# Mask rows of a query tile on ScalarE, and three weight remainders on VectorE, both instead of GpSimd

## The chip, the core and the metric

One NeuronCore of a Trainium2 chip runs the whole kernel. The metric is the time of one execution on the device, in microseconds (us); lower is better. The engines are named as in the profile: PE is TensorE's matmul side and PEld its weight loads, DVE is VectorE, ACT is ScalarE, POOL is GpSimd and SP is SyncE, which issues most DMAs here. A q behind a name (SPq, POOLq) is that engine's instruction queue.

## What is computed

One layer of a decoder is applied to a prompt of 1024 tokens and, with the same weights, to 8 sample sequences of 4 new tokens each (32 rows). Cut to what matters here:

```python
h = rmsnorm(x, norm1_g)
q, kv, gn, u, mq, gb = in_proj(h, w_in)
# branch A: compressed blocks + selected blocks + sliding window, with ALiBi
s = einsum('bghtd,bgnd->bghtn', q, k) * dh ** -0.5 - slope * distance
o_a = gate0 * softmax(s_cmp) @ v_cmp + gate1 * softmax(s_sel) @ v_sel + gate2 * softmax(s_win) @ v_win
# branch B: state space scan; branch C: cross attention into 256 memory rows
x = x + (concat(o_a, o_b, o_c) * gb) @ w_o
def ffn(x, g, w1, w2):                 # w1: 1024 x 4096, w2: 4096 x 1024
    h = rmsnorm(x, g)
    return x + square(relu(h @ w1)) @ w2
```

The sample sequences read their selected rows out of a paged cache, through a page table. All arithmetic is fp32. A product is done as three matmuls on rounded parts: a value is split into a rounded "hi" and the remainder "lo = value - hi", and hi x hi, hi x lo and lo x hi are added up.

## The kernel before

The program is written stage by stage in Python and then put in order by a scheduler that simulates a timeline. It fixes one static order of instructions for each engine, and each engine works through its own list without overtaking, so an instruction that waits holds up all that stands behind it on the same engine.

The stages that the change touches are two.

**Attention, about 630 to 1060 us of the profile.** For each of 8 query tiles j of 128 tokens there is one unit of memory attention (`mem_unit`) and, for each of 2 key groups g, two units of prompt attention (`nsa_units`). The scores of a unit are S = QA·KA + mask + QB·KB, in the lines L839, L841 and L842. QA holds the rounded queries. QB has the remainders of the queries in its rows 0 to 63 (VectorE, L792), and in its rows 64 to 127 the mask rows that belong to the tile: constant rows `augq`, multiplied by a column of factors `augj` that selects the tile (L790). KB has the key positions in the same rows, so that the second matmul also adds the position bias. QA and QB have two buffers each, which the memory units share, so the next QB can be written only when PE has read the tile before the last one. DVE takes the row maximum (L847), ACT the exponential P (L848), DVE scales P (L880), PE transposes it (T, L893), ACT copies the transpose out (PT, L895), and PE multiplies with the values (O, L907).

Into the same stretch the scheduler weaves the attention of the sample sequences (`sample`). Its selected cache rows are gathered by indirect DMAs that POOL issues (L1338, tile `xs`, 512 KB each, 32 of them, 7 buffers), and PE transposes (L1497) and multiplies them (L1504, L1529).

**The start of the MLP, about 1220 to 1300 us.** After the output projection (L1668 adds its result into `acc`) the hidden input is split into h2hi (ACT, L1720) and h2lo (DVE, L1722), in 3 column chunks of 352 tokens by 8 slices. The MLP has 32 tiles m of 128 hidden units, 4 of them in the first group. For each m, `weights` loads one 128 x 1024 piece of w_ff1 (`raw`, 3 buffers, L1633), ACT rounds it to `hi` (L112) and L118 forms `lo`; PE computes 3 chunks of 24 matmuls each (`fps`, L122 to L124); ACT and DVE make the squared relu and split it (L1762 to L1765). A piece of w_ff2 is loaded into another `raw` buffer and split into f2hi (L112) and f2lo (L118). After m = 1, PE sums the squares of the norm (L1743), DVE rescales them (L1744), and PE transposes a part of them (L1779) before it goes on with m = 2.

The argument `e_lo` of `split` names the engine of the subtraction in L118: "pool" unless a caller says "dve". In the MLP only the w_ff1 piece of m = 0 goes to DVE; all other lo pieces of both matrices go to POOL.

Of the kernel before, what the change touches and what calls it, by code (L numbers as in the profile page):

```python
# [13 lines left out]
AF = mybir.ActivationFunctionType  # L14
ALU = mybir.AluOpType
# [8 lines left out]
KT = D // 128  # L24
# [77 lines left out]
class Build:  # L102
# [671 lines left out]
    def nsa_units(self, pool, psp, j, g):  # L774
        nc = self.nc
        ctx = {"n": 0, "total": (j + 1) + min(j + 1, 5) + 1}

        def prep():
            tk = slice(j * 128, j * 128 + 128)
            qd = pool.tile([128, 4, 128], F32, name="qd", tag="qd", bufs=3)  # L780
            for dd in range(2):
                nc.sync.dma_start(qd[dd * 64:(dd + 1) * 64], self.s_q[g * 256:(g + 1) * 256, tk].rearrange("(h d) t -> d h t", d=64))
            qd = qd.rearrange("p h t -> p (h t)")
            if g == 0:
                self._gn = pool.tile([128, 3, 8], F32, name="gn", tag="gn", bufs=2)
                nc.sync.dma_start(self._gn.rearrange("p b h -> p (b h)"), self.s_gn[tk])
            ctx["gn"] = self._gn
            QA = pool.tile([128, 512], R32, name="QA", tag="QA", bufs=2)
            QB = pool.tile([128, 512], R32, name="QB", tag="QB", bufs=2)
            nc.gpsimd.tensor_scalar(QB[64:128], self.augq[64:128, g * 512:(g + 1) * 512], self.augj[64:128, j:j + 1], None, op0=ALU.mult)  # L790
            nc.scalar.activation(QA, qd, AF.Copy, scale=0.125)
            nc.vector.scalar_tensor_tensor(QB[0:64], qd[0:64], 0.125, QA[0:64].bitcast(F32), op0=ALU.mult, op1=ALU.subtract)  # L792
            ctx["QA"], ctx["QB"] = QA, QB
            ctx["gb"] = pool.tile([128, 256], F32, name="ngb", tag="ngb", bufs=5)
            for a in range(2):
                nc.sync.dma_start(ctx["gb"][:, a * 128:(a + 1) * 128], self.s_gb[2 * g + a][:, j * 128:(j + 1) * 128])

        return [self.nsa_unit(pool, psp, j, g, b, ctx, prep if b == 0 else None, b == (0 if j < 7 else 1)) for b in range(2)]
# [925 lines left out]
    def ffn(self, rp, wp):  # L1724
        nc, A = self.nc, self.A
# [3 lines left out]
        with self.pool("ff") as pool, self.pool("ffp", PSUM) as psp:  # L1729
# [9 lines left out]
            def sum_ms():  # L1739
                for o, n in CHUNKS:  # L1740
                    cs = slice(o, o + n)
                    ps = psp.tile([128, 512], F32, name="fps", tag="fps", bufs=8)
                    nc.tensor.matmul(ps[:, :n], ones, ms[:, cs], start=True, stop=True)  # L1743
                    ts(ms[:, cs], ps[:, :n], 1.0 / D, EPS, op0=ALU.mult, op1=ALU.add)  # L1744
# [5 lines left out]
            for g0, NG in GROUPS:  # L1750
                hid = []
                for m in range(g0, g0 + NG):
                    mc = slice(m * 128, m * 128 + 128)
                    hi, lo = self.weights(wp, A["w_ff1"][0][:, mc], KT, "dve" if m == 0 else "pool")
                    yh = pool.tile([128, NT], R32, name="yh", tag="yh", bufs=4)
                    yl = pool.tile([128, NT], R32, name="yl", tag="yl", bufs=4)
                    for ci, (o, n) in enumerate(CHUNKS):
                        ps = psp.tile([128, 512], F32, name="fps", tag="fps", bufs=8)
                        for k in range(KT):
                            self.mm3(ps[:, :n], hi[:, k], lo[:, k], hhi[:, k, o:o + n], hlo[ci][:, k], k == 0, k == KT - 1)  # L1760
                        r = rp.tile([128, 512], F32, name="rl", tag="rl", bufs=2)[:, :n]
                        nc.scalar.activation(r, ps[:, :n], AF.Relu)  # L1762
                        tt(r, r, r, op=ALU.mult)  # L1763
                        nc.scalar.activation(yh[:, o:o + n], r, AF.Copy)
                        tt(yl[:, o:o + n], r, yh[:, o:o + n].bitcast(F32), op=ALU.subtract)  # L1765
                    raw2 = wp.tile([128, 8, 128], F32, name="raw", tag="raw", bufs=3)
                    hi2 = pool.tile([128, KT, 128], R32, name="f2hi", tag="f2hi", bufs=4)
                    lo2 = pool.tile([128, KT, 128], R32, name="f2lo", tag="f2lo", bufs=4)
                    nc.sync.dma_start(raw2.rearrange("p k c -> p (k c)"), A["w_ff2"][0][mc])
                    self.split(hi2, lo2, raw2)  # L1770
                    hid.append((yh, yl, hi2, lo2))
                    if m == 1:
                        sum_ms()
                        for i0 in (0, 8):
                            pm = psp.tile([128, 512], F32, name="fps", tag="fps", bufs=8)
                            r = rows(i0)
                            n = 8 if i0 == 0 else 1
                            for i in range(i0, i0 + n):
                                nc.tensor.transpose(pm[:r, (i - i0) * 32:(i - i0) * 32 + 32], ms[0:32, i * 128:i * 128 + r], ident[:32, :32])  # L1779
                            nc.vector.reciprocal(rm[:r, i0:i0 + n], pm[:r, 0:n * 32].rearrange("p (i c) -> p i c", c=32)[:, :, 0])  # L1780
                            stt(rm2[:r, i0:i0 + n], rm[:r, i0:i0 + n], 1.0 / D, rm[:r, i0:i0 + n], op0=ALU.mult, op1=ALU.mult)
                        for k in range(KT):
                            eng = nc.gpsimd if k >= 4 else nc.vector
                            eng.tensor_tensor(acc[:, k], acc[:, k], ms, op=ALU.mult)
                last = g0 + NG == 32
                steps = [(m, c) for c in LAST for m in range(KT)] if last else [(m, c) for m in range(KT) for c in CHUNKS]
                for si, (m, (o, n)) in enumerate(steps):
                    ps = psp.tile([128, 512], F32, name="fps", tag="fps", bufs=8)
                    for a, (yh, yl, h2, l2) in enumerate(hid):
                        self.mm3(ps[:, :n], h2[:, m], l2[:, m], yh[:, o:o + n], yl[:, o:o + n], a == 0, a == NG - 1)  # L1790
                    tt(acc[:, m, o:o + n], ps[:, :n], acc[:, m, o:o + n], op=ALU.add)  # L1791
                    if last and si in NORMS:
                        self.final_norm(pool, wp, psp, NORMS.index(si), rm, rm2, gf)
# [70 lines left out]
```

## Time and profile before

| | |
|---|---|
| median of 3 runs | 1992.77 us (1992.62 to 1998.18) |
| profiled execution | 1998.81 us, of which the span of the profile is 1997.0 us |
| PE busy | 1898.1 us (95%) |
| DVE busy | 1145.0 us (57%) |
| ACT busy | 754.5 us (38%) |
| POOL busy | 433.7 us (22%) |
| granted TensorE clock, mean | 0.976 of full speed |

The time of a profiled execution is its span plus about 1.8 us around it. An engine's share of the span is a mean over stages with different limits; whether its work counts is read from the stretch where it lies. "[6.66 <-DMA xs]" in a row means that the engine was idle for 6.66 us before this instruction and that a DMA into xs ended that. The granted clock has two levels that matter here, 1.2 and 2.4 GHz; in a stretch of time the profile gives the mean as a share of the higher.

### The profile page before, as it was taken

To read this page: it belongs to the slowest core of one execution; us is meant where nothing else is said; L and a number is where in the kernel's file an instruction comes from. 1 tells how busy PE (TensorE), PEld (TensorE's weight loads), DVE (VectorE), ACT (ScalarE), POOL (GpSimd) and SP (SyncE) were. 2 spreads that over 40 slices of the span, in tenths; PEclk is the share of its full clock that TensorE was granted. 3 is DMA by queue.
4 is the path that set the end of the run, shared out by engine and by line. 5 is a ranking of instruction groups with operands and counts; after the bars stand their busy time and mean duration, and the time that the engine had idled before them with its cause. 6 is when DMAs were issued, how large, how long until landed. Compare 5 with 4: busy or idle time off the path is not lost.

```text
span 1997.0 us, 33847 instructions
## 1 busy us (share of the span) xinstructions
PE 1898.1 (95%) x13280; PEld 1727.4 (86%) x13280; DVE 1145.0 (57%) x2735; ACT 754.5 (38%) x1696; POOL 433.7 (22%) x282
## 2 busy tenths in 40 slices
PE   8988999999997898989998999999999999999997
PEld 8987889999996665666657899999999999999997
DVE  6378897425535776786774226725455555544536
ACT  6301224226655666766774224212222111222222
POOL 2044431441102320022000122512121111122200
PEclk9988999999998799999999999999999999999999
DMA  7443323655336643433323223112111111111102
GB/s 267 150 132 91 102 79 102 180 178 181 117 114 136 182 143 95 144 95 108 107 75 121 70 80 96 53 32 64 43 43 53 43 43 43 43 44 52 43 1 87
DMA packets 197689, 191.31 MB, mean 96 GB/s; under 512 B 32925, under 2 KB 177046, under 8 KB 196314
## 3 DMA queue, kind: packets, MB, share of 16 engines
q1 hardware_dynamic: 190730, 153.86, 25.9%
q0 software_dynamic: 6800, 35.30, 5.3%
q8 instruction: 104, 1.70, 0.4%
q14 instruction: 55, 0.45, 0.1%
HBM read 155.34 MB, written 38.55 MB: 97 GB/s over the span
## 4 chain that ended last, share of the span: by engine, by line
PE 79%; DVE 9%; DMA 5%; issue 3%; ACT 2%; SPq 1%; POOL 1%; DVEq 0%; ACTq 0%; POOLq 0%
PE fps L122 12%; PE fps L124 12%; PE fps L123 12%; PE pso L122 4%; PE pso L124 4%; PE pso L123 4%; PE O L907 4%; PE T L893 3%; PE ops L124 2%; PE ops L122 2%; PE ops L123 2%; PE S L842 2%; PE S L839 2%; DMA xs<-cache_slc_kv,idx 1%; PE cps L632 1%
## 5 line engine op out<-in xcount | busy, mean ns | idle before, releaser
L1791 DVE TENSOR_TENSOR acc<-fps,acc 128x352 f32<-128x352 f32 (+3 forms) x336 | 173.4, 523 | 166.4 <-PE fps L124 166.3
L123 PE MATMUL fps<-h2lo,hi 128*128 128x352 f32 x768 | 249.0, 324 | 3.3 <-DVE h2lo L1722 3.3
L124 PE MATMUL fps<-h2hi,lo 128*128 128x352 f32 x768 | 249.5, 325 | 0.0
L122 PE MATMUL fps<-h2hi,hi 128*128 128x352 f32 x768 | 249.0, 325 | 0.0
L123 PE MATMUL fps<-yl,f2hi 128*128 128x352 f32 (+3 forms) x768 | 245.2, 322 | 0.0
L124 PE MATMUL fps<-yh,f2lo 128*128 128x352 f32 (+3 forms) x768 | 245.1, 322 | 0.0
L122 PE MATMUL fps<-yh,f2hi 128*128 128x352 f32 (+3 forms) x768 | 241.8, 323 | 0.0
L1763 DVE TENSOR_TENSOR rl<-rl 128x352 f32<-128x352 f32 x96 | 127.0, 1323 | 136.9 <-ACT rl L1762 136.9
L118 POOL TENSOR_TENSOR lo<-raw,hi 128x1024 fp32r<-128x1024 f32 (+1 forms) x43 | 96.8, 2252 | 378.0 <-ACT hi L112 378.0
L124 PE MATMUL pso<-hhi,wlo 128*128 128x352 f32 x480 | 157.8, 329 | 0.0
L123 PE MATMUL pso<-hlo,whi 128*128 128x352 f32 x480 | 157.6, 328 | 0.0
L122 PE MATMUL pso<-hhi,whi 128*128 128x352 f32 x480 | 157.5, 328 | 0.0
L118 POOL TENSOR_TENSOR f2lo<-raw,f2hi 128x1024 fp32r<-128x1024 f32 x32 | 77.6, 2429 | 349.9 <-ACT f2hi L112 294.4
L123 PEld LDWEIGHTS fps<-h2lo,hi 128*128 128x128 f32 x768 | 145.8, 190 | 4.1 <-DVE h2lo L1722 4.1
L848 ACT ACTIVATE P<-S,nst 128x384 f32<-128x384 f32 (+4 forms) x264 | 127.1, 488 | 57.9 <-DVE nst L847 46.8
L124 PEld LDWEIGHTS fps<-h2hi,lo 128*128 128x128 f32 x768 | 146.3, 190 | 0.0
L122 PEld LDWEIGHTS fps<-h2hi,hi 128*128 128x128 f32 x768 | 145.8, 190 | 0.1
L847 DVE TENSOR_REDUCE nst<-S 128x1 f32<-128x384 f32 (+4 forms) x264 | 109.5, 433 | 62.5 <-PE S L842 47.5
L123 PEld LDWEIGHTS fps<-yl,f2hi 128*128 128x128 f32 x768 | 144.0, 188 | 1.4
L124 PEld LDWEIGHTS fps<-yh,f2lo 128*128 128x128 f32 x768 | 143.9, 188 | 1.4
L122 PEld LDWEIGHTS fps<-yh,f2hi 128*128 128x128 f32 x768 | 143.2, 188 | 1.5
L112 ACT ACTIVATE f2hi<-raw 128x1024 fp32r<-128x1024 f32 x32 | 33.7, 1058 | 271.9 <-PE fps L123 255.6
(596 smaller groups left out, 4529.5 us busy)
## 6 DMA issues: line engine op xcount, KB each, us to landing
raw<-w_ff SPq DMA_DIRECT2D x64, 512.0 KB
wraw<-w_in SPq DMA_DIRECT2D x28, 512.0 KB
xs<-cache_mem_kv SPq DMA_DIRECT2D x16, 512.0 KB
s_gb<-st SPq DMA_DIRECT2D x36, 176.0 KB
x<-x_prompt SPq DMA_DIRECT2D x8, 512.0 KB
wraw<-w_mem_kv SPq DMA_DIRECT2D x8, 512.0 KB
qd<-s_q SPq DMA_DIRECT2D x32, 128.0 KB
ngb<-s_gb SPq DMA_DIRECT2D x64, 64.0 KB
```

The costliest lines, as they stand in the source:

```text
L118: eng.tensor_tensor(lo, src, hi.bitcast(F32), op=ALU.subtract)
L122: mm(ps, ahi, bhi, start=start, stop=False)
L123: mm(ps, ahi, blo, start=False, stop=False)
L124: mm(ps, alo, bhi, start=False, stop=stop)
L839: nc.tensor.matmul(S[:, :w], ctx["QA"][:, qs], KA[:, k0:k0 + w], start=True, stop=False)
L842: nc.tensor.matmul(S[:, :w], ctx["QB"][:, qs], KB[:, k0:k0 + w], start=False, stop=True)
L847: nc.vector.tensor_reduce(t[:, 0, pi, i:i + 1], S[:, o:o + pw], axis=AX.X, op=ALU.max, negate=True)
L848: nc.scalar.activation(P[:, o:o + pw], S[:, o:o + pw], AF.Exp, bias=t[:, 0, pi, i:i + 1], accum_out=t[:, 1, pi, i:i + 1])
L893: nc.tensor.transpose(T[:w, i * 128:(i + 1) * 128], Ps[i, si][:, o:o + w], self.ident)
L907: nc.tensor.matmul(O[c * 64:(c + 1) * 64, :256], v, pv[:w, c], start=n == 0, stop=n == total - 1)
L1763: tt(r, r, r, op=ALU.mult)
L1791: tt(acc[:, m, o:o + n], ps[:, :n], acc[:, m, o:o + n], op=ALU.add)
```

## The change

Two things move off POOL. The 16 multiplications of L790 become ACT instructions (a copy with a scale per partition). And three subtractions of L118 become DVE instructions: lo of the w_ff1 piece m = 1, and f2lo of the w_ff2 pieces m = 0 and m = 1.

```diff
@@ nsa_units, prep
-            nc.gpsimd.tensor_scalar(QB[64:128], self.augq[64:128, g * 512:(g + 1) * 512], self.augj[64:128, j:j + 1], None, op0=ALU.mult)
+            nc.scalar.activation(QB[64:128], self.augq[64:128, g * 512:(g + 1) * 512], AF.Copy, scale=self.augj[64:128, j:j + 1])
             nc.scalar.activation(QA, qd, AF.Copy, scale=0.125)
@@ ffn
-                    hi, lo = self.weights(wp, A["w_ff1"][0][:, mc], KT, "dve" if m == 0 else "pool")
+                    hi, lo = self.weights(wp, A["w_ff1"][0][:, mc], KT, "dve" if m < 2 else "pool")
@@ ffn
-                    self.split(hi2, lo2, raw2)
+                    self.split(hi2, lo2, raw2, e_lo="dve" if m < 2 else "pool")
```

The scheduler makes a new order from this for all engines in the attention stretch and at the start of the MLP; before the attention the order is the same. On POOL, in the attention stretch, with the gathers written as `DMA xs`:

```order
-L790 TENSOR_SCALAR QB<-augq,augj 64x512
-L1451 TENSOR_TENSOR xs<-xs,tri 128x900
-L1338 DMA xs<-cache_slc_kv,idx_7260 128x1024 x3
-L790 TENSOR_SCALAR QB<-augq,augj 64x512 x2
-L118 TENSOR_TENSOR w0lo<-mxr,w0hi 128x1024
-L1338 DMA xs<-cache_slc_kv,idx_7260 128x1024 x4
-L790 TENSOR_SCALAR QB<-augq,augj 64x512 x2
-L1338 DMA xs<-cache_slc_kv,idx_7260 128x1024 x8
-L790 TENSOR_SCALAR QB<-augq,augj 64x512 x2
-L1338 DMA xs<-cache_slc_kv,idx_7260 128x1024
-L790 TENSOR_SCALAR QB<-augq,augj 64x512 x2
```

These eleven rows are gone; in their place the gathers stand one behind another (13 in a row, and 16 later), with only L1451 and one w0lo between them.

On ACT, around one of the query tiles, the order before is

```order
L848 ACTIVATE P,nst<-S,nst 128x128
L791 ACTIVATE QA<-qd 128x512
L1347 ACTIVATE KTs<-sS 128x512
L895 ACTIVATE PT<-T 128x512
L895 ACTIVATE PT<-T 63x512
L791 ACTIVATE QA<-qd 128x512
L508 ACTIVATE P,nst<-S,nst 128x256 x4
```

and of the changed kernel, at the same tiles,

```order
L791 ACTIVATE QA<-qd 128x512
L790 ACTIVATE QB<-augq,augj 64x512
L848 ACTIVATE P,nst<-S,nst 128x128
L1347 ACTIVATE KTs<-sS 128x512
L895 ACTIVATE PT<-T 128x512
L895 ACTIVATE PT<-T 63x512
L791 ACTIVATE QA<-qd 128x512
L790 ACTIVATE QB<-augq,augj 64x512
```

Each L790 stands right behind the L791 of its tile (only the first tile has it ahead), and exponentials and copies out of PSUM stand behind it.

On DVE, at the start of the MLP (h2lo_14251 is the third column chunk), as a difference from before to after:

```order
 L1722 SCALAR_TENSOR_TENSOR h2lo_14251<-acc,g2c,h2hi 128x352
 L1737 MEMSET ones 128x128
+L118 TENSOR_TENSOR f2lo<-raw,f2hi 128x1024
+L118 TENSOR_TENSOR lo<-raw,hi 128x1024
+L118 TENSOR_TENSOR f2lo<-raw,f2hi 128x1024
 L1722 SCALAR_TENSOR_TENSOR h2lo_14251<-acc,g2c,h2hi 128x352
 L1674 TENSOR_TENSOR msb<-msb,rl 128x352
-L1763 TENSOR_TENSOR rl<-rl 128x352 x2
+L1763 TENSOR_TENSOR rl<-rl 128x352
+L1744 TENSOR_SCALAR msb<-fps 128x352 x2
```

The three subtractions stand behind 16 of the 17 h2lo instructions that are left after the output projection's last sums, ahead of the last one, and two of the three rescalings L1744 have moved ahead. On PE, two of the three sums L1743 now stand among the matmuls of m = 1 instead of behind them; the third, and the transposes L1779, stay behind.

## Rows read from the trace of the kernel before

**Rows 1.** Stretches 620 to 960 (sum) and 1350:1900: us, busy per engine, clock, DMA

```profile
sum 340.00, PE 308.15 PEld 218.06 DVE 248.82 ACT 223.84 POOL 68.65; mean PE 9.06 PEld 6.41 DVE 7.32 ACT 6.58 POOL 2.02
...
1350.00:1900.00 550.00, 550.00 (x3443) 550.00 (x3442) 285.33 (x433) 115.79 (x192) 115.21 (x49) 1.00 0.16 47
```

**Rows 2.** Waits of PE, 620 to 1070: us in total, times, longest

```profile
PE S L842 <- POOL QB L790: 9.5, 2, 7.2
PE S L839 <- ACT P L848: 7.4, 6, 3.4
PE O L907 <- ACT PT L895: 6.3, 10, 1.5
...
PE sS L1497 <- DMA xs<-cache_slc_kv,idx: 2.5, 3, 1.5
```

**Rows 3.** Timeline, 742 to 762: start, us, engine, line [idle before <- what ended it]

```profile
746.69 0.94 POOL L1338 DMA_INDIRECT xs<-cache_slc_kv,idx  x1 [0.30 <-PE S L842]
...
755.87 3.22 POOL L790 TENSOR_SCALAR QB<-augq,augj 64x512 fp32r<-64x512 bf16 x2 [8.24 <-issue]
...
757.49 0.63 PE L842 MATMUL S<-KB,QB 128*128 128x320 f32 x1 [7.24 <-POOL QB L790]
```

**Rows 4.** Gathers into xs, and the timeline 660 to 690

```profile
DMA to landing us min/median/max: 5.6/6.8/8.8
...
678.62 3.22 POOL L790 TENSOR_SCALAR QB<-augq,augj 64x512 fp32r<-64x512 bf16 x2 [6.66 <-DMA xs<-cache_slc_kv,idx]
```

**Rows 5.** Stretches of 10 us, columns as in the second of Rows 1

```profile
650.00:660.00 10.00, 9.11 (x55) 8.28 (x56) 7.76 (x42) 5.14 (x27) 0.00 (x0) 0.50 0.23 51
...
750.00:760.00 10.00, 2.76 (x14) 2.46 (x13) 4.00 (x13) 2.80 (x9) 3.13 (x2) 0.73 0.49 123
760.00:770.00 10.00, 10.00 (x91) 6.26 (x89) 4.83 (x14) 7.00 (x23) 0.00 (x0) 0.92 0.00 0
```

**Rows 6.** L790 (ns min/median/max), its wait for PE; ACT's L791 and its wait

```profile
L790 POOL TENSOR_SCALAR QB<-augq,augj x16: 1563/1566/1959, 629.5 to 994.0; 64x512 fp32r<-64x512 bf16 x16
...
  PE S L842: 69.0, 3
...
L791 ACT ACTIVATE QA<-qd 128x512 fp32r<-128x512 f32 x16 | 10.1, 632 | 8.1 <-PE S L839 3.6 <-DMA qd<-s_q 2.0 <-PE S L124 1.0
...
ACT QA L791 <- PE S L839: 3.6, 5, 1.5
```

**Rows 7.** Timeline of DVE and POOL, 1195 to 1300

```profile
1217.27 1.23 DVE L118 TENSOR_TENSOR lo<-raw,hi 128x1024 fp32r<-128x1024 f32 x1 [4.16 <-ACT hi L112]
...
1228.25 11.42 DVE L1722 SCALAR_TENSOR_TENSOR h2lo<-acc,g2c,h2hi 128x352 fp32r<-128x352 f32 x10
...
1240.03 2.06 DVE L1722 SCALAR_TENSOR_TENSOR h2lo<-acc,g2c,h2hi 128x352 fp32r<-128x352 f32 x4
...
1232.55 5.26 POOL L118 TENSOR_TENSOR f2lo<-raw,f2hi 128x1024 fp32r<-128x1024 f32 x2
```

**Rows 8.** Timeline of PE: first matmul of m = 0 to the first of m = 2

```profile
1227.61 0.32 PE L122 MATMUL fps<-h2hi,hi 128*128 128x352 f32 x1
...
1256.92 1.94 PE L1743 MATMUL fps<-msb,ones 128*128 128x352 f32 x6
...
1261.63 0.40 PE L1779 MATMUL fps<-ident,msb 32*128 32x32 f32 x4 [2.35 <-DVE msb L1744]
1261.96 0.43 PE L122 MATMUL fps<-h2hi,hi 128*128 128x352 f32 x1
...
1264.27 0.49 PE L124 MATMUL fps<-h2hi,lo 128*128 128x352 f32 x1
```

**Rows 9.** Stretch 1235:1240, columns as in the second of Rows 1

```profile
1235.00:1240.00 5.00, 2.77 (x9) 2.33 (x10) 5.00 (x6) 0.00 (x0) 2.80 (x2) 0.60 0.65 193
```

**Rows 10.** Load of the w_ff1 piece m = 2 issued, and its rounding on ACT

```profile
1232.62 0.38 SPq L1633 DMA_DIRECT2D raw<-w_ff  x1
...
1247.50 1.05 ACT L112 ACTIVATE hi<-raw 128x1024 fp32r<-128x1024 f32 x1
```

## The prediction

> **What bounds the kernel now.** The views are read from the coarse to the fine: the windows first, to see where PE is full and where it is not, then the waits of PE in the places where it is not, then the timeline at those waits. In the bulk of the MLP PE is busy for 550.00 of 550 us [rows 1], at about 0.160 us a matmul (550 / 3443); nothing that POOL, ACT or DVE do there can move the time. Between 620 and 960 us PE is busy for 308.15 of 340 us [rows 1], so 32 us are open, and at the start of the MLP PE waits again. The change touches just these two places. The reader should see that POOL is far from full in both (68.65 of 340 us) and still matters: not for its busy time, but because another engine stands behind it.
>
> In the attention stretch the longest single reason for PE to wait is POOL's L790: 9.5 us in two waits, of 7.2 us and 2.3 us [rows 2]. The timeline shows how the long one comes about. POOL has issued four gathers, the last at 746.69, and its next instruction is L790, which starts only at 755.87; PE stands for 7.24 us until the QB is there [rows 3]. A gather takes 5.6 to 8.8 us from issue to landing [rows 4], and 746.69 + 8.8 = 755.5: L790 starts just as the last gather is in. At 678.62 the same is said outright, L790 is released by the landing of a gather [rows 4]; this is the place of PE's other wait, the 9.5 - 7.2 = 2.3 us of [rows 2]. So L790 waits for gathers whose data it does not read, because it stands behind them on POOL.
>
> At the start of the MLP the bound is DVE, and behind it POOL. From 1228.25 ten h2lo instructions take 11.42 us, 1.14 each, where four of the same shape take 2.06, 0.51 each, a little later [rows 7]. The slow ones lie under POOL's subtractions: two f2lo run from 1232.55 for 5.26 us [rows 7]. PE waits for h2lo in that time; in 1235 to 1240 it is busy for 2.77 of 5 us, at a granted clock of 0.60, while DVE shows 5.00 of 5 [rows 9].
>
> **Part 1: L790 from POOL to ACT.** Removed are 16 instructions of 1.57 us on POOL [rows 6], 25 us that lie beside other work, and with them the two waits of PE, 2.3 + 7.2 = 9.5 us. On ACT the multiplication has no gather ahead of it. Behind the long wait PE also runs slower: the granted clock is 0.73 over 2.76 busy us and 0.92 over 10 [rows 5], which costs 0.27 x 2.76 + 0.08 x 10 = 1.5 us that goes with the wait. What is late next at these places? Behind the L842 at 757.49 PE has transposes of cache rows whose gathers are older than the four that L790 waited for, so I expect no wait of like size there. Gain: **11.0 us**, bounds 0 (another wait takes its place) and 11.0.
>
> Added are 16 instructions on ACT. The trace has none of this form there; the nearest row is L791, 632 ns for 512 columns [rows 6]. That is 16 x 0.63 = 10 us of busy time on an engine that is busy for 223.84 of 340 us [rows 1]. The Trainium skill, "ScalarE: Activation LUTs", section What ACT_TABLE_LOAD costs, gives 186 ns + 0.833 ns a column and 93 ns more for an operand of one value per partition, 0.71 us here; by it the busy time would be 11 us and the sum 0.1 to 1.4 us worse, and no row of L790 on ACT is there to check it.
>
> Each L790 also waits for PE to have read the old QB, and exponentials and copies stand behind it on ACT. On POOL that wait was 69.0 us in 3 cases and hurt nobody [rows 6]. L791 on ACT waits for the same tile's other buffer, 3.6 us in 5 cases, 1.5 at most [rows 6], and L790 stands right behind it, so most of its wait has passed by then. PE's own waits for ACT's two outputs are 7.4 + 6.3 = 13.7 us [rows 2], 6% of ACT's 223.84 busy us, so of 10 us more on ACT some 0.6 us would come through; to that I add as much again as L791 waits now, at most 3.6 us, and take 60% of it. Cost: **3 us**, bounds 0 and 10 + 3.6 = 14.
>
> POOL's queue is shorter for the gathers. That is worth little: a gather waits mostly for PE to free one of the 7 buffers. I take 0. The new order of the whole stretch is a term of its own, since the scheduler shuffles exponentials, transposes and gathers. I take 0 for it and 6 us either way, about as much as the other waits of rows 2 without ACT's larger one (6.3 + 2.5 = 8.8) could shrink or grow by two thirds.
>
> Attention: -11 + 3 = **-8 us**, from -17 to +9.
>
> **Part 2: three subtractions from POOL to DVE.** From its first matmul of m = 0 at 1227.61 to the first of m = 2 at 1261.96 PE takes 34.35 us [rows 8]. Its work there is 144 matmuls x 0.160 = 23.0 us, and 1.94 us of sums and about 0.9 us of transposes [rows 8], 25.9 in all. So 8.4 us are lost; and after the last wait, 2.35 us, matmuls of m = 2 start 0.29 us apart for about 12 instances (0.49 us each in [rows 8]) instead of 0.16, another 1.5 us. The pot is 9.9 us.
>
> With the change POOL has nothing to do there until pieces of m = 2 are split. DVE then needs 16 h2lo and 2 sums of 0.51 us, 9.2 us from 1228.25, to 1237.5. The three subtractions follow, 1.23 us each by the one that DVE did at 1217.27 [rows 7], 3.7 us, to 1241.2, and the last h2lo to 1241.7, where before it ended at 1246. PE, if it never waits, reaches the first matmul with lo of m = 1 after 76 matmuls and two sums, at 1227.6 + 12.2 + 1.3 = 1241.1, and lo is there at 1240.0; it reaches the last h2lo's matmul at about 1244, and that is there at 1241.7. So the chain just keeps up, and the third sum, its rescaling and the transposes end near 1254 instead of 1262. Cover: the raw buffers are freed later, near 1239 instead of 1232.6, so the next w_ff1 piece is loaded about 6 us later; before, it lay from 1232.62 to 1247.50 before ACT rounded it [rows 10], 15 us, so there is room. If that cover is gone, PE waits for lo of m = 2, by my count 2 us away. Gain: **8 us**, bounds 9.9 and a loss of 3.7 (see the third rival).
>
> **Sum.** -8 - 8 = -16 us against the profiled execution's own 1998.8 us: 1982.8. The median of the runs is 6.0 us under that execution. If these 6 us lie elsewhere, the median becomes 1976.8; if the quicker runs are those in which gathers land sooner and PE waits less for L790, they are part of the gain and it stays at 1982.8. I take the middle, **1980 us**.
>
> **Rivals.** First, a gather takes the place of L790. PE waits for gathers already, 2.5 us in 3 waits [rows 2], and if the prompt's tiles come sooner the transposes of cache rows do too, against an unchanged 6.8 us. Then part 1 nets about zero and part 2 remains: 1993 - 8 + 3 = 1988. For it speaks that all three waits follow the same pattern; against it, that the rows behind the long wait read older gathers.
>
> Second, slower: ACT's queue. If the wait of L790 for the old QB falls on ACT while exponentials stand behind it, PE loses it 16 times. At L791's worst wait of 1.5 us [rows 6] the price is 16 x (0.63 + 1.5) = 34 us, against a gain of 11 + 8 = 19: 2008. It decides from 19 / 16 = 1.2 us per multiplication, its own time included. For it speaks the 69.0 us of waiting on POOL; against it, that in the new order L790 stands behind L791, whose mean wait is 0.7 us in 5 of 16 cases.
>
> Third, DVE is simply full. It shows 5.00 of 5 us [rows 9]. If POOL is not what stretches h2lo, three more subtractions make the chain 3.7 us longer: -8 + 3.7, or 1989. Against it stands that h2lo takes 0.51 us wherever POOL rests and 1.14 beside it [rows 7]. The Trainium skill, "Perfetto Trace Analysis", section Optimizing Scalar/DVE Operations, advises to move work to GpSimd where DVE is saturated, and adds that the two share a port, so that moving between them might not help; by the first half this part loses 3.7 us, and these rows speak for the second half, with DVE's time stretched, not filled.
>
> Fourth, the clock gains more. The early attention runs partly at the lower level: from 650 to 660 PE is busy for 9.11 us at 0.50 of the full clock [rows 5], 4.6 us lost. If the new order leaves fewer gaps ahead of two such stretches, 9 us more are saved: 1971.
>
> That the change would not do what it says is excluded by the order: the multiplications are on ACT and the subtractions on DVE.
>
> **Chances.** Forecast 0.60; gather 0.15; ACT's queue 0.10; full DVE 0.08; clock 0.07. A measurement of this kernel can tell 0.3%, 6 us, from no change. Faster by more, under 1986.8: 0.60 + 0.07 + a fifth of the gather's case, 0.70. Slower by more, over 1998.8: 0.10. Between: 0.20. The range for 8 in 10: its lower end is the forecast less 6 us for the order and 9 us for the clock, 1965; its upper end takes in the gather's case and that of the full DVE with 3 us more of the order's term, 1992. Left out are ACT's queue and the tails.
>
> **What would show it.** Right, for part 1: no row in which PE waits for QB at more than 1 us, and gathers on POOL that follow one another; the wait of ACT's L790 for PE under 5 us in total. Right, for part 2: the ten h2lo at about 5.2 us instead of 11.4, and under 28 us between the first matmul of m = 0 and the first of m = 2. Wrong: PE's waits for P or PT from ACT grow by more than 5 us, PE waits for xs in place of QB, or POOL's pieces of m = 2 come after PE needs them.

## The result, and the profile after

The changed kernel takes 1978.49 us (median of 5 runs, 1975.86 to 1982.21) against 1992.77 us before (1991.86 to 1998.18). The medians are 14.3 us apart, a ratio of 0.9928; the ratio estimated from all runs is 0.9918, with a 95% interval of 0.9896 to 0.9939, which is 16.3 us. Ratios below are of this second kind. The forecast was 1980, from 1965 to 1992. The profiled execution took 1978.21 us, its span is 1976.4; before, span 1997.0. The two profiles differ by 20.6 us, more than the medians, because the profiled execution of before is slower than its median.

The program falls into four stretches with the same work in each kernel: the attention, from the first score matmul that reads a QB to the first matmul of the output projection; the projection; the MLP's start, from the first fps matmul of m = 0 to the first of m = 2; the rest. Here are the first and third in the windows view, of before and then of after (start:end, length, busy time and instructions of PE, PEld, DVE, ACT, POOL, granted clock, share and GB/s of DMA).

```profile
646.60:1070.00 423.40, 391.47 (x3266) 261.39 (x3263) 311.18 (x1018) 288.57 (x883) 64.10 (x50) 0.95 0.38 115
1227.61:1261.96 34.35, 28.68 (x161) 26.86 (x160) 31.56 (x37) 14.20 (x25) 18.29 (x8) 0.90 0.32 96
```

```profile
645.50:1054.10 408.60, 386.79 (x3266) 256.43 (x3265) 307.44 (x1018) 298.27 (x898) 38.06 (x34) 0.97 0.38 118
1212.18:1241.36 29.18, 25.83 (x162) 24.75 (x160) 26.11 (x39) 13.85 (x24) 8.60 (x4) 1.00 0.33 99
```

PE has the same 3266 matmuls in the attention and is done 14.8 us sooner: 10.1 us less idle (31.9 to 21.8) and 4.7 us less busy time at a higher granted clock. The MLP's start is 5.2 us shorter. The projection takes 157.6 and 158.1 us, the rest 735.04 us in both, so nothing is given back later; the last 1.1 us lie ahead of the attention.

The waits of PE in the attention of after (engine, line, waited for: us in total, times, longest), to be held against [rows 2]:

```profile
PE O L907 <- ACT PT L895: 6.1, 11, 1.2
PE T L893 <- DVE P L880: 4.6, 3, 3.2
PE S L839 <- ACT P L508: 3.2, 4, 1.3
PE S L839 <- ACT P L848: 3.0, 5, 0.8
PE sS L1497 <- DMA xs<-cache_slc_kv,idx: 2.0, 2, 1.0
```

No wait for QB is left, and the wait for P from L848 has fallen from 7.4 to 3.0 us, its longest from 3.4 to 0.8. New are 2.8 us for P from DVE's L880 (1.8 before) and 1.9 for P from L508 (1.3 before). L790 itself, in the view of one line of after (ns min/median/max, first and last start), answers [rows 6]:

```profile
L790 ACT ACTIVATE QB<-augq,augj x16: 716/717/720, 638.0 to 981.5; 64x512 fp32r<-64x512 bf16 x16
```

ACT stood idle ahead of none of the 16, and nobody waited more than 0.2 us for one.

At the MLP's start, the timeline of after (start, us, engine, line [idle before <- what ended it]) answers [rows 7 and 8]:

```profile
1212.82 5.04 DVE L1722 SCALAR_TENSOR_TENSOR h2lo<-acc,g2c,h2hi 128x352 fp32r<-128x352 f32 x10
...
1221.76 1.17 DVE L118 TENSOR_TENSOR f2lo<-raw,f2hi 128x1024 fp32r<-128x1024 f32 x1
1222.83 1.22 DVE L118 TENSOR_TENSOR lo<-raw,hi 128x1024 fp32r<-128x1024 f32 x1
1223.96 1.23 DVE L118 TENSOR_TENSOR f2lo<-raw,f2hi 128x1024 fp32r<-128x1024 f32 x1
...
1238.15 2.39 DVE L1765 TENSOR_TENSOR yl<-rl,yh 128x352 fp32r<-128x352 f32 x1 [0.80 <-ACT yh L1764]
1240.46 0.51 DVE L1744 TENSOR_SCALAR msb<-fps 128x352 f32<-128x352 f32 x1
```

```profile
1237.81 2.35 POOL L118 TENSOR_TENSOR f2lo<-raw,f2hi 128x1024 fp32r<-128x1024 f32 x1 [3.05 <-ACT f2hi L112]
```

```profile
1236.50 0.75 PE L1743 MATMUL fps<-msb,ones 128*128 128x352 f32 x2
1237.19 0.49 PE L1779 MATMUL fps<-ident,msb 32*128 32x32 f32 x5
1241.03 0.40 PE L1779 MATMUL fps<-ident,msb 32*128 32x32 f32 x4 [3.35 <-DVE msb L1744]
1241.36 0.54 PE L122 MATMUL fps<-h2hi,hi 128*128 128x352 f32 x1
```

The ten h2lo take 5.04 us instead of 11.42, the three subtractions 1.2 us each, and PE goes from m = 0 to the sums without a wait. One wait remains, and it has grown from 2.35 us [rows 8] to 3.35: the third sum's rescaling (L1744) stands on DVE behind an L1765 of 2.39 us, which lies under POOL's f2lo of m = 3 (1237.81 to 1240.16). Behind it the clock is low again, as before:

```profile
1241.36:1246.00 4.64, 4.64 (x21) 4.64 (x20) 4.64 (x2) 0.00 (x0) 4.64 (x2) 0.63 0.66 206
```

### The profile page after: what moved, and what is told of

The parts are those of the page before. It is cut to its first block, busy times and chain, and to the rows that moved or that the text cites. A ratio compares the mean times of both kernels' runs of the same rounds, so it can differ in the third digit from the quotient of the medians.

```text
span 1976.4 us, 33827 instructions
## 1 busy us (share of the span) xinstructions
PE 1889.7 (96%) x13280; PEld 1719.3 (87%) x13280; DVE 1139.4 (58%) x2738; ACT 764.8 (39%) x1712; POOL 399.1 (20%) x263
## 4 chain that ended last, share of the span: by engine, by line
PE 78%; DVE 9%; DMA 5%; ACT 3%; issue 2%; SPq 1%; POOL 1%; DVEq 0%; ACTq 0%; POOLq 0%
PE fps L122 12%; PE fps L124 12%; PE fps L123 12%; PE pso L122 4%; PE pso L124 4%; PE pso L123 4%; PE O L907 4%; PE T L893 4%; PE ops L124 2%; PE ops L122 2%; PE ops L123 2%; PE S L842 2%; PE S L839 2%; PE cps L632 1%; PE cps L122 1%
## 5 line engine op out<-in xcount | busy, mean ns | idle before, releaser
L1763 DVE TENSOR_TENSOR rl<-rl 128x352 f32<-128x352 f32 x96 | 127.0, 1324 | 134.4 <-ACT rl L1762 134.3
L118 POOL TENSOR_TENSOR lo<-raw,hi 128x1024 fp32r<-128x1024 f32 (+1 forms) x42 | 94.9, 2261 | 399.5 <-ACT hi L112 399.5
L118 POOL TENSOR_TENSOR f2lo<-raw,f2hi 128x1024 fp32r<-128x1024 f32 x30 | 71.9, 2399 | 377.0 <-ACT f2hi L112 331.3
L848 ACT ACTIVATE P<-S,nst 128x384 f32<-128x384 f32 (+4 forms) x264 | 127.9, 490 | 44.0 <-DVE nst L847 34.4
```

Source lines behind the costliest of these rows:

```text
L118: eng.tensor_tensor(lo, src, hi.bitcast(F32), op=ALU.subtract)
L848: nc.scalar.activation(P[:, o:o + pw], S[:, o:o + pw], AF.Exp, bias=t[:, 0, pi, i:i + 1], accum_out=t[:, 1, pi, i:i + 1])
```

## The experiments

Medians, ratios to the kernel before on the same chip, and the two stretches of the profiled execution:

| kernel | us (runs) | ratio, 95% | attention | m = 0 to 2 |
|---|---|---|---|---|
| before | 1991.5 to 1994.0 in four comparisons | | 423.4 | 34.3 |
| the change | 1978.5 (5) | 0.9918, 0.9896 to 0.9939 | 408.6 | 29.2 |
| part 1 alone | 1980.8 (6) | 0.9942, 0.9928 to 0.9956 | 406.1 | 34.3 |
| part 2 alone | 1988.8 (12) | 0.9977, 0.9962 to 0.9991 | 418.3 | 29.2 |
| L790 on DVE | 1991.2 (12) | 0.9985, 0.9970 to 1.0000 | 419.1 | 29.8 |
| L790 twice on ACT | 1981.8 (6) | 0.9948, 0.9928 to 0.9968 | 410.8 | 29.9 |
| POOL multiplies too | 1982.8 (6) | 0.9956, 0.9939 to 0.9973 | 411.7 | 29.5 |
| DVE multiplies too | 1975.5 (6) | 0.9919, 0.9901 to 0.9937 | 405.1 | 29.3 |
| POOL subtracts too | 1981.8 (6) | 0.9944, 0.9927 to 0.9962 | 405.8 | 34.7 |
| transposes later | 1976.2 (6) | 0.9921, 0.9904 to 0.9938 | 404.6 | 24.7 |
| backlog 12, POOL | 1989.1 (12) | 0.9979, 0.9966 to 0.9993 | 416.8 | 29.4 |
| backlog 12, ACT | 1980.5 (6) | 0.9929, 0.9915 to 0.9943 | 406.9 | 29.7 |
| backlog 16, POOL | 1990.5 (12) | 0.9985, 0.9972 to 0.9997 | 419.7 | 29.6 |
| backlog 16, ACT | 1975.7 (5) | 0.9907, 0.9891 to 0.9923 | 404.9 | 29.8 |

### Each part alone

Part 1 alone:

```diff
-                    hi, lo = self.weights(wp, A["w_ff1"][0][:, mc], KT, "dve" if m < 2 else "pool")
+                    hi, lo = self.weights(wp, A["w_ff1"][0][:, mc], KT, "dve" if m == 0 else "pool")
...
-                    self.split(hi2, lo2, raw2, e_lo="dve" if m < 2 else "pool")
+                    self.split(hi2, lo2, raw2)
```

> Part 1 alone (L790 on ACT; the three subtractions of the MLP's start back on POOL). Theory A, that the two parts do not touch each other: the stretch from the first score matmul with QB to the first matmul of the output projection takes 408.6 us as in the changed kernel (423.4 before), and from the first fps matmul of m = 0 to the first of m = 2 it takes 34.3 us as before, so about 1978.5 + 5.2 = 1983.7 us, 9 us faster than before. Rival B, that part 1 is worth only what PE lost by its two waits for QB less my price for ACT, 8 us, and part 2 the other 6 to 8: about 1985 us and a stretch of 415 us. Rival C, that the attention's gain comes and goes from run to run: the stretch lies near 416 us.

Part 2 alone:

```diff
-            nc.scalar.activation(QB[64:128], self.augq[64:128, g * 512:(g + 1) * 512], AF.Copy, scale=self.augj[64:128, j:j + 1])
+            nc.gpsimd.tensor_scalar(QB[64:128], self.augq[64:128, g * 512:(g + 1) * 512], self.augj[64:128, j:j + 1], None, op0=ALU.mult)
```

> Part 2 alone (the three subtractions on DVE; L790 back on POOL). Theory A: the stretch from m = 0 to m = 2 takes 29.2 us as in the changed kernel, the attention 423 us as before, and the time is 1992.8 - 5.2 = 1987.6 us. Rival: the 5.2 us stand in the trace but are given back later in the MLP, whose bulk is bound by PE and cannot give anything back unless a load comes late: 1990 us or more. The ten h2lo take about 5.1 us instead of 11.4 and PE has one wait there, for msb, of 3 to 3.5 us.

The parts do not touch each other. By the ratios part 1 is worth 0.58% or 11.6 us and part 2 0.23% or 4.6 us, 16.2 together; the change, 0.82%, is 16.3. By their intervals each of these is known to some 3 or 4 us. Theory A holds for part 1: its stretch is 406.1 us, and rivals B, 415, and C, 416, fall; the time is 3 us under the 1983.7 that theory A gave. In part 2 the 5.2 us of the trace arrive nearly whole. But part 2's kernel, with the instruction order of before, has an attention of 418.3 us where the profile of before had 423.4: about 5 us of that one profile are its own.

### L790 on a third engine

```diff
-            nc.scalar.activation(QB[64:128], self.augq[64:128, g * 512:(g + 1) * 512], AF.Copy, scale=self.augj[64:128, j:j + 1])
+            nc.vector.tensor_scalar(QB[64:128], self.augq[64:128, g * 512:(g + 1) * 512], self.augj[64:128, j:j + 1], None, op0=ALU.mult)
```

> As the changed kernel, but L790 on DVE instead of ACT. Theory A (L790 was late only because it stood behind gathers on POOL; any engine without gathers will do): PE has no wait for QB over 1 us, the attention stretch takes 408 to 413 us, and the time is 1977 to 1983 us. Rival B (the gain above the two waits comes from the order that the scheduler found with L790 on ACT): with another order the stretch takes 414 us or more and the time is 1984 us or more. Rival C (DVE is the tighter engine, 311 busy us of 423 against ACT's 289): PE's waits for DVE, 4.6 us in the changed kernel, grow by 5 us or more.

My theory fell here: no wait for QB is left, and yet the attention takes 419.1 us, and the time is no better than with part 2 alone. Rival B's bounds hold. Rival C's do not: PE's waits for DVE are 8.9 us, where the changed kernel has 5.3. Leaving POOL is not enough. Two groups of PE's waits in this kernel, the longest of each between 840 and 860 us:

```profile
PE S L839 <- ACT P L848: 5.0, 5, 4.0
PE sS L1478 <- DVE sPT L1475: 2.3, 1, 2.3
```

And the timeline of this kernel at the wait of 4.0 us:

```profile
841.87 2.67 POOL L1451 TENSOR_TENSOR xs<-xs,tri 128x900 f32<-128x900 f32 x1 [13.68 <-DVE xs L1450]
842.71 1.85 DVE L868 TENSOR_TENSOR nfx<-nfy,nst 128x8 f32<-128x8 f32 x1
844.59 0.21 ACT L869 ACTIVATE nfx<-nfx 128x8 f32<-128x8 f32 x1 [3.11 <-DVE nfx L868]
846.19 0.69 PE L839 MATMUL S<-KA,QA 128*128 128x384 f32 x1 [4.02 <-ACT P L848]
```

A DVE instruction of 8 columns takes 1.85 us, because it ends when POOL's L1451 ends (841.87 + 2.67 = 844.54; 842.71 + 1.85 = 844.56). The maxima of the next scores stand behind it on DVE, the exponentials behind those, and PE behind these. The kernel before has the same stall at 857, under its L1451:

```profile
853.37 2.66 POOL L1451 TENSOR_TENSOR xs<-xs,tri 128x900 f32<-128x900 f32 x1 [11.48 <-DVE xs L1450]
854.20 1.85 DVE L871 TENSOR_TENSOR nfy<-nfy 128x4 f32<-128x4 f32 x1
855.97 1.21 DVE L847 TENSOR_REDUCE nst<-S 128x1 f32<-128x256 f32 x3
...
857.04 0.68 PE L839 MATMUL S<-KA,QA 128*128 128x384 f32 x1 [3.37 <-ACT P L848]
```

In the changed kernel the same L1451 comes at 834.13, with reductions of S beside it, and they are not stretched (three of 384 columns and less in 1.01 us):

```profile
834.13 2.63 POOL L1451 TENSOR_TENSOR xs<-xs,tri 128x900 f32<-128x900 f32 x1 [73.31 <-PE T L893]
834.92 1.01 DVE L847 TENSOR_REDUCE nst<-S 128x1 f32<-128x384 f32 x3
```

So part of the gain hangs on what the scheduler puts on DVE beside one instruction of POOL. At this place the stall is there, with 3.4 us, in all four profiles with L790 on POOL, and in none with one L790 on ACT. By the rows the stretching itself makes 1.7 us of it (1.85 less 0.16); the rest is what stands ahead on DVE and the way over ACT.

L1451 runs twice, though, and the first one, near 661 us, stalls PE in the changed kernel too:

```profile
661.19 2.66 POOL L1451 TENSOR_TENSOR xs<-xs,tri 128x900 f32<-128x900 f32 x1 [18.41 <-DVE xs L1450]
662.03 1.91 DVE L880 TENSOR_SCALAR P<-P,nst 128x128 f32<-128x128 f32 x1
664.00 0.33 PE L893 MATMUL T<-ident,P 128*128 128x128 f32 x1 [3.17 <-DVE P L880]
```

L880 with 128 columns takes 0.28 us elsewhere. This is the longest wait for P from L880 in the list of the changed kernel. In the kernel before, the first L1451 stretches a small instruction as well (L863 with 4 columns, 1.32 us), and PE waits 1.8 us. The two L1451 together cost PE 5.2 us before and 3.2 us after, so at them the new order won about 2 us, not 3.4.

The Trainium skill, "SBUF — State Buffer", section Who interferes with whom, says that a DVE instruction with two inputs in SBUF contends with a GpSimd instruction that reads SBUF. These rows agree, 0.16 us against 1.85, and the reductions, with one input, go through. L880 is held up too; its inputs are one tensor and one factor per partition.

The other wait, 2.3 us, is DVE's queue: ahead of the copy that PE waits for, L1475 at 853.10, DVE has no idle time, and L790 (0.49 us), L792, L505 and L1461 (0.7 us each) stand there.

### The price on ACT

```diff
             nc.scalar.activation(QB[64:128], self.augq[64:128, g * 512:(g + 1) * 512], AF.Copy, scale=self.augj[64:128, j:j + 1])
+            nc.scalar.activation(QB[64:128], self.augq[64:128, g * 512:(g + 1) * 512], AF.Copy, scale=self.augj[64:128, j:j + 1])
```

> As the changed kernel, but ACT executes L790 twice in a row (16 more instructions of 0.72 us, 11.5 us). It prices the term for ACT, which I put at 3 us with bounds 0 and 14. Theory A (ACT has room in the attention, 298 busy us of 409): PE's waits for P and PT, 12.3 us in the changed kernel, grow by no more than 2 us and the time is 1978 to 1981 us. Rival B (my price, 3 us for 10): 1982 us. Rival C (ACT's queue is what sets the pace, so all of it comes through): 1990 us.

1981.8 us lies on the border of A and B, and rival C falls: of 11.5 us more on ACT about 5 come through (410.8 against 406.0, the mean of the five profiles in the changed order, which go from 404.6 to 408.6: the change, part 1 alone, POOL subtracts too, transposes later, backlog 16 on ACT). PE's waits for P and PT from ACT are 16.0 us. The changed kernel's profile has 12.3, but the other four in its order have 9.0 to 9.5, so they grew by 4 to 7 us and the trace speaks for B rather than A. The order is another one too, so this is a hint at the price and doesn't measure it.

### POOL's queue without the wait

```diff
             nc.scalar.activation(QA, qd, AF.Copy, scale=0.125)
+            QX = pool.tile([128, 512], R32, name="QX", tag="QX", bufs=1)
+            nc.gpsimd.tensor_scalar(QX[64:128], QA[64:128].bitcast(F32), self.augj[64:128, j:j + 1], None, op0=ALU.mult)
```

> As the changed kernel, with ACT's L790, and POOL executes 16 multiplications of the same shape besides, from QA into a tile that nobody reads. PE, DVE and ACT have instruction for instruction the order of the changed kernel; on POOL the 16 stand between the gathers much as L790 did before. So it tells POOL's queue apart from the one who waits. Theory A (what L790 cost before was PE's wait for its result; the gathers behind it did not matter): no PE wait for QB, the attention stretch stays at 406 to 411 us, the time at 1977 to 1982 us, though POOL's multiplications stand waiting for gathers as L790 did. Rival B (the gathers come sooner when POOL is free, and that made the gain beyond the two waits, some 5 us): PE's waits for xs grow from 2.0 us to 5 or more and the time is 1983 us or more.

Rival B holds: the waits for xs reach its 5 us, and the time, 1982.8 us, is 0.2 us short of its bound. With the order of PE, DVE and ACT unchanged the attention goes to 411.7 us, and its row and PE's wait for gathers are:

```profile
644.40:1056.10 411.70, 390.08 (x3266) 257.90 (x3263) 311.96 (x1018) 300.02 (x898) 68.78 (x51) 0.96 0.39 119
```

```profile
PE sS L1497 <- DMA xs<-cache_slc_kv,idx: 5.5, 4, 2.3
```

3.5 us more of waiting for xs, and DVE busy for 312.0 us instead of 307.4. The multiplications stand in POOL's queue as L790 did and hold up the gathers behind them, and they stretch DVE. In the kernels with L790 on POOL DVE is busy for 311 to 313 us too, and xs is waited for 2.5 to 4.6 us. These multiplications read fp32 and take 1.92 us (median) where L790 took 1.57, and wait for ACT's QA, not for PE. So what POOL's queue cost before is not measured by this; as an estimate, 5.7 us (411.7 less 406.0) to 7.6 us (by the ratios) is its upper end.

### DVE's load

```diff
             nc.scalar.activation(QA, qd, AF.Copy, scale=0.125)
+            QX = pool.tile([128, 512], R32, name="QX", tag="QX", bufs=1)
+            nc.vector.tensor_scalar(QX[64:128], QA[64:128].bitcast(F32), self.augj[64:128, j:j + 1], None, op0=ALU.mult)
```

> As the changed kernel, with ACT's L790, and DVE executes 16 multiplications of the same shape besides (0.49 us each, 7.8 us), from QA into a tile that nobody reads. It asks why L790 on DVE gave nothing (attention 419.1 us, no wait for QB). Theory A (DVE is the engine next to PE in the attention, 307 busy us of 409; any work on it comes through more than once): the stretch is 415 us or more and the time 1985 us or more. Rival B (it was the order that the scheduler found with L790 on DVE, by chance a worse one): the order here is another again, the stretch is as likely under 412 us as over, and a time under 1982 us speaks for B.

Theory A falls. DVE is busy for 10 us more than in the changed kernel, and the attention is as short as any:

```profile
642.20:1047.30 405.10, 385.48 (x3266) 256.63 (x3264) 317.18 (x1033) 298.92 (x898) 42.80 (x35) 0.97 0.39 120
```

So the load by itself is not what made L790 on DVE slow. Nor did L790 wait there: in that kernel's trace none of the 16 stood idle ahead of its start, and nobody waited more than 0.2 us for one. That leaves the order. No run isolates it, since the order of this kernel is another one again.

### POOL beside DVE at the MLP's start

```diff
                     hi, lo = self.weights(wp, A["w_ff1"][0][:, mc], KT, "dve" if m < 2 else "pool")
+                    lox = pool.tile([128, 2, 128], R32, name="lox", tag="lox", bufs=1)
+                    [nc.gpsimd.tensor_tensor(lox, hi[:, h:h + 2].bitcast(F32), hi[:, h:h + 2].bitcast(F32), op=ALU.subtract) for h in (0, 2, 4, 6) if m == 1]
...
                     hid.append((yh, yl, hi2, lo2))
+                    [nc.gpsimd.tensor_tensor(lox, raw2[:, h:h + 2], hi2[:, h:h + 2].bitcast(F32), op=ALU.subtract) for h in (0, 2, 4, 6) if m < 2]
```

> As the changed kernel, and at the MLP's start POOL makes three subtractions' worth of work besides (12 pieces of 128x256, two f2lo and one lo, into a tile that nobody reads). PE, DVE and ACT have the order of the changed kernel, so DVE still does the three itself. Theory A (POOL's subtractions stretch DVE's beside them): h2lo and the sums under them take 1.1 us or more again instead of 0.51, PE waits for h2lo again, and from m = 0 to m = 2 it takes 33 us or more instead of 29.2; the time is 1982 us or more. Rival B (the ten h2lo were slow before for another reason, their reads beside ACT's writes or the load of w_ff): they keep 0.51 us, the stretch keeps 29 to 30 us, the time stays at 1978.

Theory A holds. The stretch is 34.72 us again, the time 1981.8 us, and DVE's instructions are slow where POOL's pieces lie, from 1218.08 to 1229.19. Here are DVE's, and then the first of the three groups of POOL's, in the timeline:

```profile
1215.30 6.99 DVE L1722 SCALAR_TENSOR_TENSOR h2lo<-acc,g2c,h2hi 128x352 fp32r<-128x352 f32 x10
1222.21 0.93 DVE L1674 TENSOR_TENSOR msb<-msb,rl 128x352 f32<-128x352 f32 x1
1223.06 3.61 DVE L1722 SCALAR_TENSOR_TENSOR h2lo<-acc,g2c,h2hi 128x352 fp32r<-128x352 f32 x4
```

```profile
1218.08 3.82 POOL L1771 TENSOR_TENSOR lox<-raw,f2hi 128x256 fp32r<-128x256 f32 x4 [18.31 <-ACT f2hi L112]
```

Four h2lo take 3.61 us there, 2.07 in the changed kernel, and PE waits for h2lo again, 1.6 us. The bound of 1.1 us an instruction that I had set is missed (0.9), since POOL's pieces are a quarter as long and leave gaps.

### The wait that was left

```diff
                     if m == 1:
                         sum_ms()
+                        for k in range(KT):
+                            eng = nc.gpsimd if k >= 4 else nc.vector
+                            eng.tensor_tensor(acc[:, k], acc[:, k], ms, op=ALU.mult)
+                    if m == 2:
                         for i0 in (0, 8):
...
-                        for k in range(KT):
-                            eng = nc.gpsimd if k >= 4 else nc.vector
-                            eng.tensor_tensor(acc[:, k], acc[:, k], ms, op=ALU.mult)
```

> As the changed kernel, but the nine small transposes of msb (L1779), for which PE waited 3.35 us, are issued after the matmuls of m = 2 instead of before them. Theory A (that wait and the slow clock behind it are all that is left of the pot at this place): PE has no wait from m = 0 to m = 2, the first matmul of m = 2 starts 25 us after the first of m = 0 (29.2 less 3.35 and the transposes), the matmuls of m = 2 start 0.16 us apart at once, and the time is 1978.5 - 3.35 - 1.5 = 1973.6 us. Rival B (PE then waits for the pieces of m = 2 or for room in PSUM because DVE is late): a wait of 2 us or more comes right behind, and the time stays at 1977 to 1979.

The multiplications of `acc` stay behind m = 1, so that they now stand ahead of the transposes. From m = 0 to m = 2 PE now works without a gap, at the full clock, and then it waits elsewhere:

```profile
1209.17:1233.82 24.65, 24.65 (x152) 24.12 (x151) 22.52 (x36) 11.37 (x21) 5.04 (x2) 1.00 0.31 95
```

```profile
PE fps L122 <- ACT yh L1764: 3.1, 1, 3.1
```

The wait for yh comes behind the first of w_ff2's matmuls and ends at 1262.71. From the first matmul of m = 0 to the end it takes 24.65 + 740.68 = 765.3 us, in the changed kernel 29.18 + 735.04 = 764.2. So rival B holds in substance, with its wait at a later place than I had put it. What stands there, in the timelines of DVE, POOL and PE:

```profile
1246.91 6.97 DVE L1776 TENSOR_TENSOR acc<-acc,msb 128x1056 f32<-128x1056 f32 x2
1257.84 2.38 POOL L118 TENSOR_TENSOR lo<-raw,hi 128x1024 fp32r<-128x1024 f32 x1 [5.07 <-ACT hi L112]
1258.14 2.46 DVE L1763 TENSOR_TENSOR rl<-rl 128x352 f32<-128x352 f32 x1 [0.40 <-ACT rl L1762]
1262.71 0.66 PE L122 MATMUL fps<-yh,f2hi 128*128 128x352 f32 x1 [3.10 <-ACT yh L1764]
```

ACT makes yh out of what DVE's L1763 writes. DVE is late with L1763 because multiplications of `acc` (L1776) stand ahead of it, and the one at 1258.14 takes 2.46 us instead of 0.52, under POOL's next lo. In this trace, then, DVE and POOL are the bound of the first group of four tiles, and the wait of PE that was taken away in its midst came back at its end. The median, 1976.2 us, lies between the two forecasts; by the ratio, 0.9921 against 0.9918, nothing was gained.

### Another order

`self.backlog` is set to 12 or 16 instead of 14, in pairs with L790 on POOL and on ACT (the edit of part 2 alone, and the change).

```diff
-        self.backlog = 14
+        self.backlog = 12
```

> Part 2 alone with self.backlog = 12 instead of 14: the prompt's attention keeps 12 deferred transposes and products waiting instead of 14, so the scheduler finds another order for the whole attention; L790 is on POOL. With its partner on ACT it asks whether the worth of part 1 hangs on one order. Theory A (who waits, and the gathers behind: a cost in every order): PE waits for QB again, 5 us or more, and the attention stretch is 10 to 18 us longer than the partner's. Rival B (the order decides, as when L790 on DVE gave 419.1 us): the stretch can be shorter than the partner's; the difference lies anywhere between -10 and +15 us.

> The changed kernel with self.backlog = 12 instead of 14; L790 is on ACT. Theory A: no wait for QB, the attention stretch 10 to 18 us shorter than that of the partner with L790 on POOL. Rival B: any difference between -10 and +15 us.

> Part 2 alone with self.backlog = 16, a third order; L790 is on POOL. Theory A: PE waits for QB, 5 us or more, and the attention stretch is 10 to 18 us longer than that of the partner on ACT. Rival B: any difference between -10 and +15 us.

> The changed kernel with self.backlog = 16; L790 is on ACT. Theory A: no wait for QB, the attention stretch 10 to 18 us shorter than that of the partner with L790 on POOL. Rival B: any difference between -10 and +15 us. If the time is under 1974 us it is a version better than the changed kernel.

At 12 the order is another one in part: in the traces of the attention some 400 of 3300 matmuls of PE stand elsewhere, and none of POOL's instructions. PE waits 8.3 us for QB with L790 on POOL and not at all on ACT:

```profile
645.40:1062.20 416.80, 390.14 (x3265) 260.36 (x3264) 312.71 (x1018) 287.98 (x883) 64.31 (x50) 0.95 0.39 116
```

```profile
648.00:1054.90 406.90, 384.27 (x3265) 253.76 (x3263) 308.67 (x1017) 300.10 (x898) 37.96 (x34) 0.98 0.39 118
```

The difference is 9.9 us, just under theory A's 10 and within rival B's bounds, and 8.6 in the medians. For A speaks that 8.3 of it are the wait for QB. At 16 I had expected a third order, but that backlog gave back the orders of 14 (but for one transpose on PE of the POOL kernel). Its pair are repetitions: 419.7 against 404.9 us, 1990.5 against 1975.7. So part 1 gains at both settings, by 9 to 15 us, with the wait for QB in each kernel on POOL and in none on ACT. That the order alone decides is not what these show. But the two settings have POOL's list in common, and no run has L790 on ACT in the order of before, so a very different order stays untried for this pair of engines.

## Why the prediction was right, and where not

**The time.** 1980 was forecast, 1978.5 measured, and the sum of -16 us is -16.3 by the ratio. The halves were not: -8 and -8 were forecast, about -12 and -4.6 measured. Part 1 was taken too small and part 2 too large, and the two errors cancel: that the sum fits so well is luck. By the medians the change is worth 14.3 us. In the profiles the attention is 14.5 us shorter on average (420.5 us in the three with before's order, which are before, part 2 alone and backlog 16 on POOL; 406.0 in the five with the changed one), 3 us more than part 1's ratio says; these are single executions, and that of part 1 alone is 3.2 us quicker than its median.

**Part 1, the wait for QB.** The step was right. 9.5 us [rows 2] are gone, and repetitions of before's order show 8.6 and 7.5 us, so the term is 8.5 rather than 9.5 on average. PE waits for no QB at more than 1 us, and the gathers follow one another on POOL, as it said. What is late next was put right too: no wait of like size for xs.

**Part 1, the clock.** Forecast 1.5 us, measured 3.5 (PE's busy time is 391.1 us on average in the three profiles with before's order and 387.6 in the five with the changed one). From 720 to 780 us the granted clock goes from 0.94 to 1.00, and from 840 to 900 from 0.97 to 1.00: I had counted the stall at QB alone; from 840 to 900, where the one at 857 lies, there was a slow stretch as well.

**Part 1, gathers.** I took 0 for POOL's shorter queue. That step failed: PE's wait for xs is 3.7 us on average in the three profiles and 2.0 in the five, and with POOL multiplying beside, 5.7 us of attention came back.

**Part 1, ACT.** I priced one L790 at 0.63 us from L791's row and the whole at 3 us, from 0 to 14. The instruction takes 0.717, 11.5 us in all. The Trainium skill, "ScalarE: Activation LUTs", section What ACT_TABLE_LOAD costs, gave 0.71, and the trace agrees. Its wait for the old QB, from which the slower rival drew its 34 us, is 0 in 16 cases. What comes through can't be separated here: doubled, it cost some 5 us in another order, so 3 may be low, and no run gives the size. Two slips in the working: the 6% sets waits of 620 to 1070 us against ACT's busy time of 620 to 960, which changes the term by 0.1 us; and the upper end of the attention's range, +9, takes the gain at its full 11 us, though its own lower bound was 0, which gives +20.

**Part 1, the order.** A term of 0 with 6 us either way. It came out at about -4.2 us for the wait for P from L848 (6.7 us on average before, 2.5 after) and +4.8 us for the waits for P from L880 and L508, 1.4 of them at the first L1451. The first has a cause that could have been read from the trace of before: the 3.4 us in [rows 2] were already there as the longest wait for P, and I had treated them as ACT's, whereas ACT waited for DVE, and half of it was DVE held up by POOL's L1451. My own argument of part 2, that POOL's two-input work stretches DVE's, would have found it. The order of the kernel with L790 on DVE shows the other side of this term, 13 us longer than the changed kernel's with the QB wait gone, beyond the 6 that I had allowed.

**Part 2.** The first wait was right: h2lo at 0.50 us, the chain in time, POOL's pieces of m = 2 not late. The second was not: "the third sum, its rescaling and the transposes end near 1254" means 26.4 us from m = 0 to m = 2, and 29.2 were measured. The step took it that with POOL idle until m = 2 the end of the stretch would be free of it. But POOL's f2lo of m = 3 falls just there, stretches L1765, and the third L1744 stands behind it. The gain is 5.2 us in the trace instead of 8. The slow clock behind the wait, which the 8 us did not count, stayed as well (0.63 over 4.64 us, 1.7 us). In the experiment with later transposes the wait of 3.35 us came back further on, so moving the transposes does not win it.

**Rivals.** The gathers did not take L790's place, ACT's queue did not set the pace (it decides from 1.2 us per multiplication; 0.717 and no wait were measured), and DVE was not simply full: with POOL made to subtract beside it the stretch went back from 29.2 to 34.7 us, with DVE's own work the same. The clock gained 2 us more than forecast, not 9.

**Left open.** The price of 16 instructions on ACT by itself; what the new order alone is worth, since no run has L790 on ACT in the order of before; and why the order with L790 on DVE has 4 us more of busy PE time. None has a run that isolates it.

## What to carry to other kernels

An engine that issues gathers should make nothing small that the busiest engine waits for: here an operand of 1.6 us came 7 us late, and the gathers behind it were late as well. Read a wait to its end: where PE waits for ACT and ACT for DVE, look at what another engine does at that moment, since a 4-column instruction of 1.85 us shows a stall that no busy share tells of. And with a scheduler that re-orders, a move between engines has a term for the order as large as the gain; repeat it in another order before you believe its size.

## What the runs showed of the hardware

While POOL's L1451 or L118 ran, which read SBUF, DVE instructions with two inputs in SBUF were held up, however small: 0.16 us became 1.85, 0.53 became 2.4. So was L880, with one tensor and one factor per partition: 0.28 us became 1.91. They ended with POOL's instruction or up to 0.4 us after it. Reductions of S with one input took their usual time beside the same L1451. The cost reached PE over DVE and ACT: a wait of 3.4 to 4.0 us at one POOL instruction of 2.66, of which the stretching makes 1.7. A copy of 64x512 from bf16 with one multiplier per partition took 1.57 us on POOL, 0.717 on ACT and 0.486 on DVE.
